# Reordering the filler projections of a hybrid RWKV-7 / neighbourhood-attention / MoE block on one Trainium2 core

## Chip, cores and metric

The kernel runs on one core of one Trainium2 chip. The metric is device time in microseconds of one execution; the median of three runs is compared. The engines are named as in the profile: PE (TensorE, matmul), PEld (its weight loads), DVE (VectorE), ACT (ScalarE), POOL (GpSimd), SP (SyncE, which here only issues DMAs).

## What is computed

One encoder layer on 512 tokens of width 1024, in float32:

```
h = rmsnorm(x)
p = h @ w_in                       # 1024 x 5504: r k v and low-rank columns of RWKV, q k v of attention, gate logits
y_a = rwkv7_bidirectional(...) @ w_o_rwkv      # 8 heads of 64, both directions
y_b = neighbourhood_attention_2d(q, k, v) @ w_o_na   # 8 heads of 64, grid 8 x 64, windows 8 x 16
x = x + (sig(g_a) * y_a + sig(g_b) * y_b) @ w_out
x = x + moe(rmsnorm(x))            # top group of 4, top 2 of its 8 experts, 32 experts
```

q and k of the attention are normalised per head (a root mean square over 64 columns, times a gain) before they are used. v and the gate logits are not.

## The kernel before, in words

**Stages.** Normalisation and the first projections; RWKV for head group 0 (`prep(0)`, which ends with the inversion of a 32x32 triangular system per chunk, `invert`), the chain of 16 chunk steps of group 0 (`chain(0)`); the same for group 1; neighbourhood attention in 8 blocks (two halves of the heads, 4 column blocks, each worked in two halves `hh`); the gated output projections (`out_gated`, `out_rows`); routing; 16 passes over pairs of experts. The experts' weights, 96 matrices of 1 MB, are loaded from the output projection on.

**The projections.** `w_in` is cut into 43 column tiles of 128. Fifteen are for RWKV. The other 28 are "others" (line 762), numbered m: 0 to 3 are q, 4 to 7 are k, 8 to 11 are v, 12 to 27 are gates. `proj` (line 304) makes one: a 512 KB weight load on SP, a split of the weights into a high and a low part (ACT writes w_hi, POOL or DVE writes w_lo; two buffers of each), and 24 matmuls of 128x512 (three for each of 8 slices) into one PSUM bank, called mm or x. Then comes what the kind of the tile asks for:

- q and k, `na_qk` (line 779): ACT squares the bank (osq) and copies it (oth), PE sums by heads into bank x, DVE takes a reciprocal square root in some twelve small operations (ngx, nrs_i, nst), spreads it (osq), PE transposes it into bank x, DVE multiplies, SP stores the tile to DRAM (d_q, d_k).
- v, `na_v` (line 800): ACT copies in three pieces, PE transposes into bank x, ACT copies, SP stores (d_v).
- gates: one ACT Tanh (oth<-mm,hb), SP stores (d_oth), line 559.

**What sets the order.** A tile framework schedules the program at compile time: each engine gets its instructions in one fixed order. The matmuls of these 28 tiles are given the lowest priority (`LOW`), what follows them the highest. Among themselves they come in the order of the program text, since weight buffers and banks are handed out in that order. `OTH` says how many are written where, `others(n)` (line 762) writes the next n: OTH[4] just ahead of the first inversion (line 745), OTH[0] after `prep(0)` (749), then the six inputs of RWKV group 1 (`GIN`, 751), OTH[1] ahead of the first chain (752), OTH[2] after the second inversion, alternating two banks (759), one after each of the first OTH[3] blocks of attention (835), and what is left after the attention, again in two banks (836).

**Who uses the results.** The attention fetches q, k and v of one half of the heads from DRAM (`na_inputs`, line 818), and its first products go into bank x (line 871), which is a single buffer. The output projection fetches the RWKV output ya, the attention output yb and the gates from DRAM; for its first 24 products (`add(m, c, range(2))`, line 961) it needs neither the second half of the heads nor the gates.

Of the kernel before, what the change touches and what calls it, by code (L numbers as in the profile page):

```python
# [23 lines left out]
HB = C // 2  # L24


OTH = (5, 8, 2, 10, 3)
GIN = [("k", 2), ("r", 2), ("v", 2), ("k", 3), ("r", 3), ("v", 3)]
WARM = 12
NX = 2  # L30
# [151 lines left out]
class K:  # L182
# [550 lines left out]
    def rwkv(self):  # L733
# [7 lines left out]
        def inputs(nm, q):  # L741
            self.rwkv_input(nm, q)
            if (nm, q) == ("v", 1):
                self.rwkv_lora(2, LOW)
                self.others(OTH[4])

        for _ in self.prep(0, inputs):
            pass
        self.others(OTH[0])
        for nm, q in GIN:  # L750
            self.rwkv_input(nm, q, LOW // 2)
        self.others(OTH[1])
        self.chain(0)
# [3 lines left out]
        for _ in p:  # L757
            pass
        self.others(OTH[2], ("mm", "x"))


    def others(self, n, banks=("mm",)):

        self.pbanks = banks
        for m in range(self.done, min(self.done + n, 28)):
            ps = self.proj(15 + m, LOW)
            t = self.rp.tile([P, T], F32, name="oth", tag="oth", bufs=2)
            with self.low(-LOW):
                if m < 8:
                    self.na_qk(m, ps, t)  # L770
                elif m < 12:
                    self.na_v(m, ps, t)
                else:
                    self.act(t, ps, AF.Tanh, scale=0.5, bias=self.hb[:, 4 + m:5 + m])
                    self.gate[m - 12] = self.spill(t, "oth%d" % m)
            self.done += 1
        self.pbanks = ("mm", "x")
# [50 lines left out]
    def na_attention(self):  # L828
        self.yb = [self.dram.tile([P, 2, 4, P], F32, name="d_yb%d" % i) for i in range(2)]
        for h4 in range(2):  # L830
            self.na_inputs(h4)
            for b in range(4):
                self.na_block(h4, b)
                if 4 * h4 + b < OTH[3]:
                    self.others(1)
# [616 lines left out]
```

## Time and profile before

| | |
|---|---|
| runs | 930.82, 932.72, 933.47 us; median 932.72 us |
| the profiled execution | 931.2 us |
| its span, first to last instruction | 929.4 us |
| mean granted clock of TensorE | 0.949 |
| busy: PE, DVE, ACT, POOL | 814.1, 433.4, 308.9, 181.5 us |

The times of stages in the trace: first inversion about 125 to 160 us, first chain 153 to 268 us, preparation of group 1 to 358 us, second inversion 358 to 390 us, second chain 383 to 490 us, attention 427 to 526 us, output projection from 562 us, experts from 685 us.

How to read the profile: "busy" is the time in which an engine has an instruction running; PE's durations are modelled, so a busy PE is not PE at its peak. A wait is idle time of an engine just before an instruction, with the instruction that ended it; "issue" is idle time for which the trace shows no releaser. The granted clock is a share of 2.4 GHz: 1.00 is that level and 0.50 the 1.2 GHz level, and a mean between is a mix in time of the two.

### The profile page before, as it was taken

The page shows a single profiled execution, that of the slowest core. Times are in us where ns is not written, and L with a number is a line of the kernel's source. Part 1 is how long each engine was busy: PE and PEld are TensorE (multiplying, and loading weights), DVE is VectorE, ACT ScalarE, POOL GpSimd, SP SyncE. Part 2 cuts the span into 40 slices and gives each one's busy share as a digit, 9 for nine tenths or more (in the row PEclk, how much of TensorE's full clock was granted, in tenths as well). Part 3 has the DMA queues.
Part 4 walks back from the last instruction along what each step waited for, and adds up shares of the span by engine and source line. Part 5 has one row for each costly group of instructions (what it writes and reads, how often), then busy time and mean ns, then how long its engine had stood idle before and what let it go on. Part 6 is the DMA issues. An engine that isn't in the chain of part 4 may idle for free. (4 is left out here: it accounts for less than half of the span.)

```text
span 929.4 us, 17293 instructions
## 1 busy us (share of the span) xinstructions
PE 814.1 (88%) x7192; PEld 529.8 (57%) x7192; DVE 433.4 (47%) x870; ACT 308.9 (33%) x667; POOL 181.5 (20%) x161
## 2 busy tenths in 40 slices
PE   8999887889987987799999999999669999888784
PEld 7676555556666765566666677878533333333331
DVE  5798984565689587224436505643612111111010
ACT  6454531123433553034756722223211111111110
POOL 2611121120003142123312230003321121211010
PEclk9999996899999999599999999999779999999998
DMA  6311130212112311422224548889989999999982
GB/s 216 110 59 47 35 102 26 68 58 69 36 59 81 125 53 62 140 72 67 81 68 137 182 135 287 300 326 380 353 330 410 394 345 395 395 393 400 398 341 44
DMA packets 49263, 176.18 MB, mean 190 GB/s; under 512 B 7584, under 2 KB 14368, under 8 KB 37152
## 3 DMA queue, kind: packets, MB, share of 16 engines
q1 hardware_dynamic: 43936, 164.56, 48.1%
q0 software_dynamic: 5248, 10.50, 4.2%
q8 instruction: 57, 0.93, 0.4%
q14 instruction: 22, 0.18, 0.1%
HBM read 159.30 MB, written 24.12 MB: 197 GB/s over the span
## 5 line engine op out<-in xcount | busy, mean ns | idle before, releaser
L203 PE MATMUL G<-ws,xT 128*64 128x512 f32 x512 | 128.9, 600 | 5.1 <-DMA ws<-in_wgu 3.8
L203 PE MATMUL mm<-hT_hi,w_lo 128*128 128x512 f32 x264 | 113.9, 432 | 7.9 <-ACT oth L188 6.8
L191 POOL TENSOR_TENSOR w_lo<-w_raw,w_hi 128x1024 fp32r<-128x1024 f32 x29 | 70.6, 2436 | 237.2 <-ACT w_hi L188 213.8
L203 PE MATMUL mm<-hT_hi,w_hi 128*128 128x512 f32 x264 | 112.0, 424 | 0.0
L203 PE MATMUL mm<-hT_lo,w_hi 128*128 128x512 f32 x264 | 111.2, 421 | 0.0
L203 PEld LDWEIGHTS G<-ws,xT 128*64 128x64 f32 x512 | 44.5, 138 | 77.7 <-issue 65.3
L203 PE MATMUL Yd<-ws,hT 128*64 128x512 f32 x256 | 65.7, 606 | 9.7 <-ACT y L188 8.7
L188 ACT ACTIVATE w_hi<-w_raw 128x1024 fp32r<-128x1024 f32 x59 | 62.2, 1055 | 30.5 <-PE mm L203 29.4
L203 PEld LDWEIGHTS mm<-hT_hi,w_lo 128*128 128x128 f32 x264 | 51.9, 197 | 26.2 <-issue 15.3
L191 DVE TENSOR_TENSOR w_lo<-w_raw,w_hi 128x1024 fp32r<-128x1024 f32 x30 | 37.7, 1257 | 50.1 <-ACT w_hi L188 50.1
L203 PEld LDWEIGHTS mm<-hT_lo,w_hi 128*128 128x128 f32 x264 | 51.8, 196 | 12.7 <-issue 2.0
L203 PEld LDWEIGHTS mm<-hT_hi,w_hi 128*128 128x128 f32 x264 | 52.0, 197 | 11.3 <-issue 1.5
L191 DVE TENSOR_TENSOR sg<-sg,G 128x256 f32<-128x256 f32 x16 | 6.7, 421 | 96.9 <-ACT sg L188 96.9
L1382 POOL DMA_INDIRECT out<-y,idx x16 | 25.2, 1577 | 117.3 <-DVE y L198 100.4
L198 DVE TENSOR_SCALAR y<-Yd,wts 128x512 f32<-128x512 f32 (+1 forms) x16 | 11.7, 734 | 77.1 <-PE Yd L203 62.6
L188 ACT ACTIVATE sg<-G,wts 128x256 f32<-128x256 f32 x16 | 7.6, 474 | 118.0 <-PE G L203 118.0
L651 DVE COPY R<-c 32x128 f32<-32x128 f32 x64 | 18.7, 293 | 52.6 <-ACT R L188 52.0
L203 PE MATMUL c<-R,T 128*32 128x64 f32 (+1 forms) x992 | 36.8, 233 | 7.2 <-DVE nrs_i L194 2.2
L203 PEld LDWEIGHTS c<-R,T 128*32 128x32 f32 (+1 forms) x992 | 26.6, 126 | 26.3 <-issue 14.0
L203 PE MATMUL tp<-T,KB 64*64 64x128 f32 x512 | 35.2, 281 | 7.3 <-ACT T L188 7.1
L203 PEld LDWEIGHTS Yd<-ws,hT 128*64 128x64 f32 x256 | 16.6, 136 | 43.5 <-ACT y L188 21.6
L188 ACT ACTIVATE T<-tp 64x256 f32<-64x256 f32 x64 | 23.9, 378 | 44.6 <-DVE T L191 43.6
(313 smaller groups left out, 1474.5 us busy)
## 6 DMA issues: line engine op xcount, KB each, us to landing
ws<-in_wgu SPq DMA_DIRECT2D x64, 1024.0 KB, 21.1
ws<-in_wd SPq DMA_DIRECT2D x30, 1024.0 KB, 21.2
w_raw<-in_w_in SPq DMA_DIRECT2D x43, 512.0 KB, 3.6
d_oth<-oth SPq DMA_DIRECT2D x16, 256.0 KB, 2.0
w_raw<-in_wo SPq DMA_DIRECT2D x8, 512.0 KB, 3.9
w_raw<-in_w_out SPq DMA_DIRECT2D x8, 512.0 KB, 5.9
x_in<-in_x SPq DMA_DIRECT2D x4, 512.0 KB, 5.4
ga<-d_oth SPq DMA_DIRECT2D x8, 256.0 KB, 4.0
```

Source lines behind the costliest of these rows:

```text
L188: self.nc.scalar.activation(out, in_, func, **kw)
L191: (eng or self.nc.vector).tensor_tensor(out, a, b, op=op)
L198: self.nc.vector.tensor_scalar(out, a, s1, None, op0=op0)
L203: return self.nc.tensor.matmul(out, l, r, start=start, stop=stop, **kw)
L651: self.nc.vector.tensor_copy(R[u, :, blk, p2], ps[u, 2:4])
L1382: self.nc.gpsimd.indirect_dma_start(out=self.A["out"], out_offset=bass.IndirectOffsetOnAxis(ap=idx, axis=0), in_=y, in_offset=None, bounds ...
```

## The change

The order of the 28 tiles is given by a list, and the five numbers differ: nine gates (12 to 20) first, then q, k and v (0 to 11), then the last seven gates. Written ahead of the first inversion: 3 as before; after `prep(0)`: 6 in place of 5; ahead of the first chain: 7 in place of 8; after the second inversion: 5 in place of 2; one after each of the first 7 blocks of attention in place of 8 blocks and 2 after it. So before, the places hold q0-q2; q3, k4-k7; v8-v11, g12-g15; g16, g17; g18-g25; g26, g27. After, they hold g12-g14; g15-g20; q0-q3, k4-k6; k7, v8-v11; g21-g27; none.

```diff
-OTH = (5, 8, 2, 10, 3)
+OTH = (6, 7, 5, 7, 3)
+
+TURN = list(range(12, 21)) + list(range(12)) + list(range(21, 28))
...
     def others(self, n, banks=("mm",)):
 
         self.pbanks = banks
-        for m in range(self.done, min(self.done + n, 28)):
+        for m in TURN[self.done:self.done + n]:
             ps = self.proj(15 + m, LOW)
```

## Rows read from the trace of the kernel before

**Rows 1.** The page, its second part: the granted clock of TensorE in 40 equal slices of the span, in tenths (9 is 90% or more).
```profile
PEclk9999996899999999599999999999779999999998
```

**Rows 2.** Busy time by stretch: the stretch and its length in us, then busy us and count of instructions of PE, PEld, DVE, ACT and POOL, the mean granted clock, the mean busy share of the DMA engines, GB/s.
```profile
125.00:160.00 35.00, 25.18 (x611) 18.65 (x609) 19.46 (x61) 7.88 (x14) 2.60 (x2) 0.78 0.20 70
145.00:165.00 20.00, 15.69 (x423) 11.98 (x425) 6.26 (x18) 3.44 (x7) 2.36 (x1) 0.50 0.13 42
165.00:227.00 62.00, 54.51 (x634) 37.51 (x634) 35.08 (x105) 17.47 (x42) 7.09 (x3) 0.97 0.18 57
290.00:358.00 68.00, 57.47 (x538) 42.35 (x537) 49.50 (x83) 33.61 (x82) 18.77 (x10) 0.95 0.25 79
358.00:397.00 39.00, 27.61 (x643) 20.14 (x646) 19.45 (x40) 6.31 (x12) 8.26 (x12) 0.69 0.34 111
370.00:390.00 20.00, 11.49 (x541) 9.71 (x542) 7.42 (x8) 1.47 (x3) 3.63 (x8) 0.50 0.50 162
397.00:427.00 30.00, 28.62 (x349) 19.12 (x342) 7.75 (x23) 10.37 (x25) 7.14 (x3) 1.00 0.25 80
526.00:562.00 36.00, 32.86 (x142) 25.95 (x140) 6.51 (x5) 10.58 (x16) 11.82 (x5) 1.00 0.50 163
```

**Rows 3.** Waits of PE from 125 to 160 us: who waited for whom, us in total, times, longest us.
```profile
PE c L203 <- issue: 5.4, 4, 2.3
PE x L206 <- DVE TI L191: 2.6, 1, 2.6
PE x L203 <- ACT osq L188: 1.1, 2, 0.7
```

**Rows 4.** The same from 160 to 227 us.
```profile
PE c L203 <- DVE nrs_i L194: 2.2, 1, 2.2
PE x L206 <- DVE osq L410: 2.1, 1, 2.1
PE c L203 <- DVE nrs_i L191: 1.5, 1, 1.5
...
PE x L203 <- ACT osq L188: 0.7, 1, 0.7
```

**Rows 5.** The same in four later stretches: the first row from 290 to 358 us, the next two from 358 to 397, the fourth from 397 to 427, the last from 526 to 562.
```profile
PE x L206 <- ACT oth L188: 2.6, 4, 0.8
...
PE c L203 <- DVE MT L605: 4.8, 1, 4.8
...
PE mm L203 <- ACT oth L188: 1.8, 2, 0.9
...
PE mm L203 <- ACT oth L188: 1.4, 2, 0.9
...
PE mm L203 <- ACT oth L188: 2.7, 3, 0.9
```

**Rows 6.** Busy time by stretch again, of the instructions alone that write or read the tile nrs_i: DVE, then granted clock, DMA share, GB/s.
```profile
160.00:227.00 67.00, 16.76 (x56) 0.93 0.19 60
```

**Rows 7.** ACT's copies of X, one in each step of a chain: first those from 160 to 227 us, then those from 397 to 427 us. Count, shortest/median/longest ns, first and last start, shape.
```profile
L188 ACT ACTIVATE X<-c x9: 277/277/278, 169.2 to 221.3; 128x128 f32<-128x128 f32 x9
...
L188 ACT ACTIVATE X<-c x5: 268/277/278, 403.1 to 423.9; 128x128 f32<-128x128 f32 x5
```

**Rows 8.** The tile oth: ACT's reads of q, k and v tiles, its reads of gates in bank mm, and SP's later fetches of the first eight gates. Columns as in rows 7.
```profile
L188 ACT ACTIVATE oth<-mm x20: 208/491/592, 116.0 to 342.3; 128x512 f32<-128x512 f32 x8, 128x64 f32<-128x64 f32 x8, 128x384 f32<-128x384 f32 x4
...
L188 ACT ACTIVATE oth<-mm,hb x14: 667/687/688, 360.6 to 561.6; 128x512 f32<-128x512 f32 x14
...
L563 SPq DMA_DIRECT2D ga<-d_oth x8: 319/327/549, 529.4 to 601.0; - x8
```

**Rows 9.** The attention's products of q and k. Columns as in rows 7.
```profile
L203 PE MATMUL x<-kT,qT x128: 218/272/373, 426.9 to 509.7; 64*128 64x128 f32 x96, 64*128 64x64 f32 x32
```

**Rows 10.** PE in order of time: the first matmul of two gate tiles beside the second chain, with one tile between them. Start us, us, engine, line, operation, out<-in, idle time before.
```profile
398.80 0.47 PE L203 MATMUL mm<-hT_hi,w_lo 128*128 128x512 f32 x1 [0.87 <-ACT oth L188]
...
417.01 0.50 PE L203 MATMUL x<-hT_hi,w_lo 128*128 128x512 f32 x1
```

**Rows 11.** In order of time, of several engines: the store of the last attention block, the end of its split on DVE, the first product of the output projection, the first two requests for expert weights. Columns as in rows 10.
```profile
526.27 0.56 SPq L907 DMA_DIRECT2D d_yb<-yb  x1
...
532.85 2.42 DVE L191 TENSOR_TENSOR yb_lo<-yb_f,yb_hi 128x256 fp32r<-128x256 f32 x1 [3.12 <-ACT yb_hi L188]
...
562.39 0.50 PE L203 MATMUL mm<-ya_lo,w_hi 128*128 128x512 f32 x1 [0.83 <-ACT oth L188]
...
564.94 0.91 SPq L1269 DMA_DIRECT2D ws<-in_wgu  x2
```

**Rows 12.** In order of time, of DVE and POOL: the start of the first inversion, a split of weights on POOL and the operation of the inversion that it met, and the like in the second inversion.
```profile
128.07 0.18 DVE L191 TENSOR_TENSOR pr<-NT,TI 128x30 f32<-128x30 f32 x1
...
133.43 2.40 POOL L191 TENSOR_TENSOR w_lo<-w_raw,w_hi 128x1024 fp32r<-128x1024 f32 x1 [9.73 <-ACT w_hi L188]
...
133.46 2.52 DVE L191 TENSOR_TENSOR pr<-NT,TI 128x126 f32<-128x126 f32 x1
...
362.59 2.37 DVE L191 TENSOR_TENSOR TI<-TI,pr 128x126 f32<-128x126 f32 x1
```

## The prediction, before the changed kernel was run

> **What bounds the kernel now.** I read the slices of the page first: TensorE (PE) is busy in nine tenths or more of almost every slice up to the expert part, and the granted clock of TensorE leaves full speed in three places, the two inversions and the routing [rows 1]. So in the part that the change touches, from about 93 us (the first projection of q) to 562 us (the first product of the output projection), PE is the bound, and what can be won there is idle time of PE and time at the lower clock. The table by stage [rows 2] shows where these are. Beside the second chain alone (397 to 427) PE is busy 28.62 of 30 us, and in the last 36 us before the output projection 32.86, with VectorE (DVE) busy only 6.51: there it works off the last gates and nothing else. The two inversions are the poor stages: 25.18 of 35 us and 27.61 of 39 us, at mean clocks of 0.78 and 0.69; from 145 to 165 and from 370 to 390 the granted clock was 0.50, which is the 1.2 GHz level.
>
> Then I read PE's waits stage by stage. From 125 to 227 us they are mostly ended by the small vector work of the q and k tiles: osq and nrs_i are the normalisation of a q or k tile [rows 3, 4]. With tiles that have no such work (v from 290 on, gates from 358 on), PE waits for ScalarE to read the one bank, oth, about 0.5 to 0.9 us a tile, and once 4.8 us in the second inversion for MT [rows 5]. DVE spends 16.76 us from 160 to 227 on the tile nrs_i alone, for some six q and k tiles [rows 6]: 2.8 us each, stretched by GpSimd. The chain shows the same: nine steps lie between 169.2 and 221.3 us, 6.5 us a step; five lie between 403.1 and 423.9, 5.2 us a step, with gates beside them [rows 7].
>
> **What the change moves.** All 28 projections stay, with all their matmuls, weight loads, splits and stores; only order and places in the program text change. The matmuls have the lowest priority, so the split into places decides little by itself: the tiles flow in their written order into whatever PE has free, through one queue of weight buffers. Before, q and k are read out from 116 us, the v tiles up to 342.3, and gates from 360.6 to 561.6 [rows 8]. After, nine gates come first, then the six inputs of the second group, then q, k, v, and the last seven gates beside the attention.
>
> Term 1, q and k leave the first inversion and chain: the waits on osq and nrs_i go, 1.1 and 2.2 + 2.1 + 1.5 + 0.7, so **-7.6 us** [rows 3, 4]. The 2.6 us on TI I don't count: PE would then stand at MT, as in the second inversion [rows 5]. What is late next there is the inversion itself on DVE. It starts at 128.07 [rows 12], and before it DVE worked on a q tile; an earlier start helps only if PE has nothing else, so zero, hidden by the projections beside it; if these ran out it would be worth up to the 2.8 us of a tile.
>
> Term 2, gates in their place: ScalarE's read ends 1.4 us of waits in 397 to 427, over three tiles, 0.47 each; eight tiles give **+3.7 us** [rows 5].
>
> Term 3, clock: from 165 to 227 it was 0.97 on the mean, so 3.7 us at the lower level, which cost about half their work, **-1.7 us**; bounds 0 and -1.7 [rows 2].
>
> Term 4, seven q and k tiles into 290 to 397, where v and gates stand now. The trace has no such tile there. The nearest rows give 0.55 us a tile (1.1 us for two tiles in the first inversion) and 1.27 (7.6 for six) [rows 3, 4]; I take 0.9, since DVE has 18.5 of 68 us idle from 290 to 358 [rows 2] and takes the 2.8 us a tile only with delay. That is 6.3 us, less the 2.6 and 1.8 us that PE waits there for oth now [rows 5]: **+1.9 us**, bounds -0.6 and +4.5.
>
> Term 5, one k and four v tiles beside the second chain in place of gates: v waits 2.6 us over four tiles against 1.4 for the gates [rows 5], **+1.2 us**. Two banks in turn instead of one save such a wait for every other tile and cost it for the next, since v itself uses bank x for its transposes: zero.
>
> Term 6, no gates after the attention: of the three waits of 0.9 us in 526 to 562 I drop two [rows 5], **-1.8 us**. The six tiles worked off there don't become free, they cost PE the same 5.7 us each earlier.
>
> The queues: 28 weight loads and stores on SP keep their spacing; the gates' stores come early and are read only from 529.4 on [rows 8], at no cost, with all of the chain between. The stores of the last q, k and v tiles now come just before SP's fetches of qT, kT and vtok; before, v's last tile was read out at 342.3 and the attention began at 426.9 [rows 8, 9]. Each fetch waits for its store, and behind it on SP stand the weight loads of the gates. Bounds 0 and 8 us; I take 0, because the projections of the chain and the chain itself cover it. The splits on GpSimd number the same.
>
> The start of the attention moves: it needs bank x, which the last tile written ahead of it holds. That was the 18th of the 28 and is now the 21st. Two tiles beside the chain started at 398.80 and 417.01 with one between, 9.1 us a tile [rows 10]; three more are 27 us, so about 454, less what is won before, 450. PE does the same work in another order, so I count nothing, with the chain's later steps as the cover; if the attention itself should end last, this is the price (second rival).
>
> Sum: -7.6 + 3.7 - 1.7 + 1.9 + 1.2 - 1.8 = **-4.3 us**. What follows 562 shifts with it: the first expert weights are requested at 564.94, just after the last gate [rows 11]. The profiled execution took 931.2 us (span 929.4 and 1.8 around it), the median of the runs shown is 932.72, 1.5 more; 931.2 - 4.3 + 1.5 = **928.4 us**. Its own range, by the bounds, is 924 to 933.
>
> **A rule that speaks against it.** Beside the first inversion an operation of 128x126 took 2.52 us while a split of weights ran on GpSimd from 133.43 for 2.40 us; in the second the same happened at 362.59 (2.37) [rows 12]. The page "SBUF — State Buffer" of the Trainium skill, section "SBUF: two separate sides", says that a DVE operation with two SBUF inputs and a GpSimd one that reads SBUF exclude each other, the later one blocking until the other ends; the trace agrees. By that rule one more split beside each inversion would add two such blocks, some 2.1 us each, and the sum would be about 0. I count none, since the number of splits that fall into an inversion follows from how fast PE works off tiles, not from the text.
>
> **Rivals.** (a) No change: the waits move with the tiles. Term 4 at its upper bound and term 3 at zero: -7.6 + 3.7 + 4.5 + 1.2 - 1.8 = 0, 932.7 us. For it: DVE is busier from 290 to 358 (0.73) than from 165 to 227 (0.57) [rows 2]. Against: the second part of the chain there has its own slack.
>
> (b) Slower: the attention ends last. It took from 426.9 to the last store at 526.27, 99 us [rows 9, 11]. From 454 it ends at 553; with a fetch of 8 us and the three further gates taking 3 us of it, 564. The last block must then go through DRAM and be split, which took from 526.27 to 535.27, 9 us [rows 11]; the output projection has 24 products that don't need it, about 6 us at 36 us for 142 matmuls [rows 2, 11]. So it decides from where the last store comes after 559 (562.39 + 6 - 9): at 564 it costs 5 to 6 us, 938.5 us. For it: 142 matmuls, six gates of 24, cover this tail now [rows 2], few or none after. Against: PE would have finished the gates by then, so the attention would have PE to itself.
>
> (c) Faster by far: the inversions fill. If gates keep PE busy where it stood at MT (4.8 us) and at TI (2.6) [rows 3, 5] and the clock stays up in both stretches of 20 us (busy 15.69 and 11.49 us at half speed, so up to 13 us; I take half, since small matmuls remain) [rows 2], this gives a further 14 us, 914.5 us. Against: in the second inversion gates were already there, and PE stood all the same, its queue being in order; 5.4 us of the first are ended by issue, not by missing work. The page "TensorE: Matmul & The Clock Gate", section "What's actually happening", of the Trainium skill says that the clock follows how busy PE has been; the trace agrees, with 0.50 granted right after these idle stretches.
>
> That the change does not do what it says is part of (a): the low priority can let the tiles run at nearly the old times.
>
> **How the numbers follow.** Forecast 0.42, (a) 0.24, (b) 0.20, (c) 0.14. About 0.3% (2.8 us) is what a measurement of this kernel can tell from no change. Faster: three quarters of the forecast, all of (c), a tenth of (a), 0.48. Same: the rest of the forecast, most of (a), a tenth of (b), 0.30. Slower 0.22. The range reaches half into (c) and past (b): 916 to 940.
>
> **What the profile of after should show.** No wait of PE ended by nrs_i or osq before 227 us; first-chain steps near 5.2 us; the q and k work of DVE between 270 and 400; in the second inversion still a wait on MT; the attention's first product at 440 to 455; its last store before 559; and the output projection's first product at about 558. A first chain that stays at 6.5 us a step, or a last store after 559, would prove me wrong.

## The result, and the profile after

The changed kernel took 941.83 us, the median of four runs (940.18 to 947.41), beside 933.1, the median of four, for the kernel before: a ratio of 1.0116, 95% interval 1.0074 to 1.0158. So it is slower by 1.2%; 928.4 had been predicted, in 916 to 940. Its profiled run is its slowest: 947.41 us, 5.6 over its median, so what the two traces differ by (16.2 us) is about twice what the medians do (8.7). Runs over 1.5% above the fastest of their kernel (two of "six gates 18, DVE splits", one of "before, low q/k") count in the medians below, but not in the ratios. In the changed kernel lines up to 27 keep their numbers, those behind stand two further down (L203 is L205).

First the granted clock, to be laid beside [rows 1]: the low slice of the first inversion (6 in the seventh place, at 139 us) is now an 8; the one slice of 5 in the second inversion (372 to 395 us) has become a trough: of the six slices from 284 to 426 us one shows 8 and four show 7.

```profile
PEclk9999898999998797779999999999969999999999
```

Busy time by stretch in the changed kernel, columns as in [rows 2].

```profile
125.00:160.00 35.00, 26.42 (x655) 19.34 (x653) 17.48 (x41) 6.90 (x14) 4.78 (x2) 0.85 0.23 78
145.00:165.00 20.00, 17.46 (x380) 12.03 (x380) 5.32 (x13) 6.19 (x14) 4.35 (x2) 0.89 0.21 69
165.00:227.00 62.00, 59.52 (x702) 38.80 (x702) 25.14 (x58) 22.49 (x52) 7.59 (x4) 1.00 0.25 82
290.00:358.00 68.00, 59.39 (x505) 43.03 (x504) 50.07 (x129) 27.60 (x55) 13.23 (x9) 0.90 0.12 40
358.00:397.00 39.00, 26.94 (x641) 19.79 (x640) 17.70 (x45) 4.46 (x11) 6.21 (x10) 0.65 0.26 84
...
397.00:427.00 30.00, 23.07 (x227) 16.57 (x226) 15.57 (x43) 6.76 (x16) 4.73 (x2) 0.83 0.18 62
526.00:562.00 36.00, 36.00 (x204) 25.87 (x202) 14.35 (x29) 26.19 (x73) 10.65 (x18) 1.00 0.37 117
```

The first chain gained what it should: PE is busy 59.52 of 62 us at full clock (54.51 at 0.97 before). The loss stands in the second inversion and above all in the second chain: 23.07 of 30 us at 0.83, where PE had 28.62 at 1.00.

Three long stretches sum this up. The same view, first of the kernel before, then of the changed one:

```profile
93.00:270.00 177.00, 154.24 (x2057) 107.89 (x2059) 119.27 (x293) 60.19 (x130) 21.22 (x14) 0.90 0.18 58
270.00:430.00 160.00, 135.24 (x1896) 98.69 (x1884) 96.14 (x179) 58.37 (x134) 39.23 (x26) 0.90 0.27 86
430.00:526.00 96.00, 90.59 (x1069) 63.98 (x1058) 47.95 (x110) 64.64 (x191) 23.30 (x45) 1.00 0.33 99
```

```profile
93.00:270.00 177.00, 156.75 (x2299) 110.01 (x2299) 107.82 (x211) 66.20 (x136) 28.51 (x18) 0.95 0.22 71
270.00:430.00 160.00, 130.57 (x1503) 95.58 (x1504) 99.53 (x251) 47.68 (x107) 28.84 (x22) 0.81 0.20 66
430.00:526.00 96.00, 89.15 (x1063) 62.19 (x1061) 37.77 (x92) 48.18 (x142) 24.68 (x31) 0.95 0.32 96
```

How to read them: idle time of PE is the length less its busy time; time at the 1.2 GHz level is twice the length times what the clock lacks to 1 (at a mean of 0.81, 2 x 160 x 0.19 = 61 us). Up to 270 us the change wins 2.5 us of idle time and 18 us of low clock; from 270 to 430 it loses 4.7 and 29, from 430 to 526 it loses 1.4 and 10. The price of a microsecond at low clock can be had from two kernels of one order: the fastest version found below starts the output projection at 534.07 us, the kernel before at 562.39 [rows 11]. In these stretches it has 13.6 us less idle time and 37 us less low clock (its rows are below); (28.3 - 13.6) / 37 = 0.4, an estimate. With it the change gains 10 us up to 270 us, loses 16 in the next stretch and 5 in the third: 12 us. From 526 to 562 us it wins 3 back (PE busy 36.00 us against 32.86), so the estimate accounts for some 9 of the 15.9 us by which its output projection starts later; the rest is open.

PE's waits in the changed kernel: from 125 to 160 us, from 160 to 227, from 358 to 397 and from 397 to 430.

```profile
PE c L205 <- issue: 3.7, 3, 1.8
PE c L205 <- DVE MT L607: 3.4, 1, 3.4
PE mm L205 <- ACT oth L190: 1.2, 2, 0.9
...
PE c L205 <- DVE R L193: 3.1, 5, 0.6
...
PE c L205 <- issue: 5.2, 3, 2.4
PE c L205 <- DVE nst L196: 3.3, 1, 3.3
...
PE c L205 <- DVE nst L202: 3.1, 1, 3.1
PE c L205 <- DVE R L653: 2.9, 1, 2.9
```

Beside [rows 3, 4]: before 227 us no wait on osq or nrs_i is left. The waits on nst, the same normalisation, now stop the products of the second inversion and chain (bank c).

The copies of X, one a step, in the same two stretches as [rows 7]:

```profile
L190 ACT ACTIVATE X<-c x12: 267/272/278, 162.9 to 222.2; 128x128 f32<-128x128 f32 x12
...
L190 ACT ACTIVATE X<-c x3: 278/278/278, 400.3 to 421.2; 128x128 f32<-128x128 f32 x3
```

The first chain's steps: 59.3 us for eleven, 5.4 each (6.5 before). The second's: 20.9 us for two, 10.4 each (5.2 before). All 16 copies of the second chain, before and after:

```profile
L188 ACT ACTIVATE X<-c x16: 256/277/278, 383.3 to 484.7; 128x128 f32<-128x128 f32 x16
...
L190 ACT ACTIVATE X<-c x16: 277/278/302, 375.1 to 488.2; 128x128 f32<-128x128 f32 x16
```

So the second chain starts 8.2 us earlier than before, takes 113.1 us instead of 101.4, and ends 3.5 us later. Beside it stand the last three of the four k tiles, as their stores show, and all four v tiles:

```profile
394.72 0.33 SPq L800 DMA_DIRECT2D d_k<-oth  x1
...
409.72 0.32 SPq L800 DMA_DIRECT2D d_k<-oth  x1
...
426.32 0.32 SPq L800 DMA_DIRECT2D d_k<-oth  x1
```

The attention's products of q and k, as in [rows 9]:

```profile
L205 PE MATMUL x<-kT,qT x128: 218/272/576, 467.4 to 556.3; 64*128 64x128 f32 x96, 64*128 64x64 f32 x32
```

And in order of time, as in [rows 11], the store of its last block, the first product of the last gate tile, and the first of the output projection:

```profile
566.11 0.51 SPq L909 DMA_DIRECT2D d_yb<-yb  x1
...
571.79 0.47 PE L205 MATMUL mm<-hT_hi,w_lo 128*128 128x512 f32 x1 [0.87 <-ACT oth L190]
...
578.30 0.50 PE L205 MATMUL mm<-ya_lo,w_hi 128*128 128x512 f32 x1 [0.83 <-ACT oth L190]
```

The attention starts 40.5 us later than before, the output projection 15.9. One of the long steps of the second chain, from 400.34 to 407.70, in order of time over the engines:

```profile
400.34 0.28 ACT L190 ACTIVATE X<-c 128x128 f32<-128x128 f32 x1 [3.08 <-PE c L205]
...
400.67 0.60 ACT L190 ACTIVATE osq<-mm 128x512 f32<-128x512 f32 x1
401.16 0.59 ACT L190 ACTIVATE oth<-mm 128x512 f32<-128x512 f32 x1
...
401.64 1.06 ACT L190 ACTIVATE w_hi<-w_raw 128x1024 fp32r<-128x1024 f32 x1
...
402.73 0.27 ACT L190 ACTIVATE R<-c 32x128 f32<-32x128 f32 x1
402.78 2.39 POOL L193 TENSOR_TENSOR w_lo<-w_raw,w_hi 128x1024 fp32r<-128x1024 f32 x1 [11.70 <-ACT w_hi L190]
...
402.82 2.37 DVE L202 TENSOR_SCALAR nst<-nrs_i 128x8 int32<-128x8 int32 x1
...
406.43 0.30 DVE L653 COPY R<-c 32x128 f32<-32x128 f32 x1
...
407.36 0.29 DVE L653 COPY R<-c 32x128 f32<-32x128 f32 x1
...
407.70 0.45 PE L205 MATMUL c<-R,T 128*64 128x64 f32 x8 [2.93 <-DVE R L653]
```

Three things stand between the chain's X and its R: on ACT the k tile's two reads and the next tile's w_hi; on DVE an operation of eight columns that began 0.04 us after GpSimd's split and ended with it; behind it the tile's remaining small operations. PE worked on a tile meanwhile, ran out at 404.8, and stood 2.93 us.

### The profile page after: what moved, and what is told of

Same layout as the page of the kernel before. It is cut to its first block, busy times and chain, and to the rows that moved or that the text cites. A ratio compares the mean times of both kernels' runs of the same rounds, so it can differ in the third digit from the quotient of the medians.

```text
span 945.6 us, 17302 instructions
## 1 busy us (share of the span) xinstructions
PE 828.3 (88%) x7192; PEld 536.3 (57%) x7192; DVE 426.6 (45%) x870; ACT 310.2 (33%) x667; POOL 181.1 (19%) x161
## 5 line engine op out<-in xcount | busy, mean ns | idle before, releaser
L205 PE MATMUL G<-ws,xT 128*64 128x512 f32 x512 | 129.9, 601 | 5.8 <-DMA ws<-in_wgu 4.4
L205 PE MATMUL mm<-hT_hi,w_lo 128*128 128x512 f32 x264 | 113.3, 429 | 4.0 <-ACT oth L190 3.7
L205 PE MATMUL mm<-hT_hi,w_hi 128*128 128x512 f32 x264 | 112.8, 427 | 0.0
L205 PE MATMUL mm<-hT_lo,w_hi 128*128 128x512 f32 x264 | 111.7, 423 | 0.0
L205 PEld LDWEIGHTS G<-ws,xT 128*64 128x64 f32 x512 | 44.6, 138 | 79.3 <-issue 65.0
L205 PE MATMUL Yd<-ws,hT 128*64 128x512 f32 x256 | 65.7, 606 | 9.7 <-ACT y L190 8.6
L205 PEld LDWEIGHTS mm<-hT_hi,w_lo 128*128 128x128 f32 x264 | 51.9, 196 | 18.2 <-issue 5.2
L205 PEld LDWEIGHTS mm<-hT_hi,w_hi 128*128 128x128 f32 x264 | 51.9, 196 | 13.2 <-issue 3.2
L205 PEld LDWEIGHTS mm<-hT_lo,w_hi 128*128 128x128 f32 x264 | 51.6, 195 | 12.0 <-issue 2.0
L205 PE MATMUL c<-R,T 128*32 128x64 f32 (+1 forms) x992 | 37.7, 236 | 13.5 <-DVE R L653 4.9
L205 PE MATMUL tp<-T,KB 64*64 64x128 f32 x512 | 41.6, 310 | 7.2 <-ACT T L190 7.2
L205 PEld LDWEIGHTS c<-R,T 128*32 128x32 f32 (+1 forms) x992 | 27.5, 129 | 35.7 <-DVE R L653 14.1
L205 PEld LDWEIGHTS tp<-T,KB 64*64 64x64 f32 x512 | 33.6, 153 | 18.3 <-ACT T L190 11.7
```

Of the source, the lines that this page charges most:

```text
L205: return self.nc.tensor.matmul(out, l, r, start=start, stop=stop, **kw)
```

## The experiments

All 18 further kernels, of 5 to 12 runs each, beside the two. The ratio is to the kernel before on the same chip, with its interval. PE's busy time and the clock are read from the profiled run, in stretches as above; the last column is the attention's first product.

| kernel | median us | ratio | PE busy, clock 93-270 | 270-430 | attention |
|---|---|---|---|---|---|
| before | | 1 | 154.2, 0.90 | 135.2, 0.90 | 426.9 |
| after | 941.8 | 1.0116 (1.0074-1.0158) | 156.8, 0.95 | 130.6, 0.81 | 467.4 |
| six gates, 18 ahead | 922.0 | 0.9912 (0.9888-0.9936) | 158.6, 0.95 | 135.6, 0.89 | 419.3 |
| three gates, 18 ahead | 926.2 | 0.9972 (0.9944-1.0001) | 157.1, 0.94 | 141.5, 0.90 | 416.1 |
| six gates, 21 ahead | 933.0 | 1.0043 (1.0015-1.0071) | 156.5, 0.94 | 137.0, 0.90 | 439.9 |
| old order, 21 ahead | 933.2 | 1.0027 (1.0005-1.0049) | 149.0, 0.91 | 137.5, 0.90 | 444.2 |
| gates, v first, 21 ahead | 932.8 | 1.0045 (1.0016-1.0075) | 157.0, 0.95 | 138.9, 0.86 | 471.2 |
| after, no rsqrt | 929.5 | 0.9986 (0.9965-1.0006) | 157.8, 0.95 | 139.7, 0.85 | 453.5 |
| before, no rsqrt | 926.3 | 0.9965 (0.9939-0.9991) | 157.2, 0.91 | 136.8, 0.91 | 421.4 |
| after, low q/k | 927.7 | 0.9993 (0.9970-1.0016) | 157.1, 0.95 | 140.9, 0.85 | 461.5 |
| before, low q/k | 929.2 | 0.9962 (0.9930-0.9995) | 153.0, 0.87 | 135.9, 0.93 | 429.3 |
| six gates 18, low q/k | 928.2 | 0.9977 (0.9957-0.9996) | 157.8, 0.93 | 134.0, 0.84 | 439.5 |
| six gates 21, low q/k | 943.7 | 1.0157 (1.0127-1.0187) | 155.6, 0.89 | 134.5, 0.85 | 455.9 |
| after, DVE splits | 913.2 | 0.9818 (0.9787-0.9849) | 159.2, 0.93 | 139.6, 0.93 | 440.9 |
| before, DVE splits | 911.8 | 0.9782 (0.9755-0.9808) | 159.4, 0.96 | 139.4, 0.90 | 408.2 |
| six gates 18, DVE splits | 913.7 | 0.9775 (0.9728-0.9821) | 160.1, 0.95 | 144.3, 0.95 | 406.3 |
| six gates 21, DVE splits | 930.6 | 1.0005 (0.9987-1.0022) | 157.8, 0.93 | 133.8, 0.87 | 443.9 |
| after, pieces | 923.8 | 0.9927 (0.9904-0.9951) | 156.7, 0.95 | 135.8, 0.88 | 449.9 |
| before, pieces | 912.7 | 0.9803 (0.9773-0.9833) | 155.5, 0.91 | 144.4, 0.96 | 408.9 |
| before, DVE splits and pieces | 902.8 | 0.9695 (0.9674-0.9717) | 161.4, 0.95 | 143.0, 0.96 | 399.2 |

**Order and places.** The theories that the expectations name: L, the attention starts late, behind 21 tiles instead of 18; Q, the q and k work now lies beside the second inversion and chain. The edits, on the kernel after, in short:

```diff
+TURN = [12..17] + [0..11] + [18..27]   # six gates first; three gates: [12..14] + [0..11] + [15..27]
 OTH = (5, 8, 2, 10, 3)                 # 18 ahead, as before
-OTH = (5, 8, 2, 10, 3)
+OTH = (6, 7, 5, 7, 3)                  # 21 ahead, as after: with six gates, or with the old order
+TURN = [12..20] + [8..11] + [0..7] + [21..27]   # gates, v first: then q, k
```

Six gates, 18 ahead: 

> Six gates first, then q, k, v, then ten gates, with the five numbers of the kernel before: 18 tiles stand ahead of the attention, the same 18 as before, only their order differs. Theory L (late attention: what costs is that 21 tiles instead of 18 stand ahead of the attention, whose first product slid from 427 to 467 us): the attention begins at 420 to 430 us again and the time is that of before, 933 us, or a little under, since the first chain keeps its 5.1 us a step. Theory Q (what costs is where the q and k work falls: beside the preparation of group 1, the second inversion and the second chain): as slow as the changed kernel, 938 to 943 us, and second-chain steps next to a k tile of 8 to 13 us.

Old order, 21 ahead: 

> The five numbers of the changed kernel with the natural order of the tiles (q, k, v, gates): 21 tiles ahead of the attention, q and k beside the first chain as before. Theory L: 940 to 943 us, the attention's first product some 25 to 40 us later than 427. Theory Q: 931 to 935 us, as before, although the attention begins later; second-chain steps near 5.2 us.

Six gates, 21 ahead: 

> Six gates first, then q, k, v, then ten gates, with the five numbers of the changed kernel: 21 tiles ahead of the attention, but q and k come three tiles earlier than in the changed kernel. Theory Q (what costs is q and k work that reaches the second inversion and the second chain): no q or k tile lies there, so the time stays near that of the same order with 18 ahead, 922 to 926 us, with second-chain steps near 5.2 us until the attention joins. Theory L (the late attention costs, and costs more with gates first): 932 us or more.

Gates, v first, 21 ahead: 

> The changed kernel with the four v tiles ahead of q and k: nine gates, v, q, k, seven gates. So four more q and k tiles reach the second inversion and chain, none fewer stand ahead of the attention. Theory Q: slower than the changed kernel, by 2 to 4 us for each of these four tiles as far as it shows, 945 to 957 us; more second-chain steps of 8 to 13 us. Theory L: as the changed kernel, 938 to 943 us, since the attention waits for the same 21 tiles.

Three gates, 18 ahead: 

> Three gates first, then q, k, v, then thirteen gates, with the five numbers of the kernel before: q and k leave the first inversion but stay beside the first chain. Theory Q and the prediction's first term (the first chain gains by having no q and k beside it): between before and six gates first, 924 to 930 us; first-chain steps 6 to 7 us once q begins, as before. If only the first inversion counts: as six gates first, 921 to 923 us.

The old order with 21 ahead came out as Q expected, six gates with 21 ahead as L did, three gates within 924 to 930; six gates with 18 ahead (922.0) and v first (932.8) are faster than either theory had it. Gates ahead of q and k are good by themselves: 0.9912 with six of them, a third of that with three. 21 tiles ahead cost 0.3% in the old order and 1.3% with six gates. Against Q: with v ahead of q, more q and k tiles lie beside the second chain than after the change, and this kernel is the faster of the two (1.0045), although its attention starts at 471.2. Its second chain takes as long (355.7 to 466.9 us), but starts 19 us earlier. So neither the count of q and k tiles there nor the late attention alone gives 1.2%.

**The q and k work itself.** In two kernels the eleven small operations of the reciprocal square root are left out, so q and k are scaled by something else; in four others the work behind a q or k tile is no longer scheduled ahead of everything.

```diff
-        self.rsqrt_bits(st, x, shape, "nrs_i")
+        st = x                                   # no rsqrt
...
-            with self.low(-LOW):
+            with self.low(LOW // 4 if m < 8 else -LOW):   # low q/k
```

After, no rsqrt: 

> The changed kernel without the eleven small vector operations of the reciprocal square root of each q and k tile (q and k are scaled by the mean square itself). To be compared with the kernel before with the same left out. Theory Q: most of the loss of 9 us is gone, so 929 to 934 us, and within 3 us of its counterpart; no step of the second chain over 8 us. Theory L: still some 8 us slower than its counterpart, attention still from 450 us or later.

Before, no rsqrt: 

> The kernel before without the same eleven small vector operations of each q and k tile. Both theories: a little faster than before, 926 to 931 us, by the waits of TensorE on nrs_i and osq beside the first chain (some 7 us by the trace of before) as far as they lie on the path. It is the counterpart from which the other kernel without them is measured.

After, low q/k: 

> The changed kernel with the epilogues of q and k tiles (copies, sums, reciprocal root, scaling, store) at a low instead of the highest priority, so that the chain's own copies are placed ahead of them. Theory Q in its sharper form (a k tile costs because its work stands in the engines' queues ahead of the chain's step): second-chain steps beside k tiles fall from 8 to 13 us to 6 to 8, time 930 to 936 us. If the cost is the work itself, or the blocking of VectorE by GpSimd, the time stays at 938 to 943 us. Theory L: no change or slower, as q and k are finished later and the attention with them.

Before, low q/k: 

> The kernel before, order and places untouched, with the same lower priority of the q and k tiles' vector work alone. Theory Q: the first chain's steps fall from 6.5 to about 5.2 us and its end comes 10 to 20 us earlier; time 924 to 930. Theory L: the attention's first product stays within 10 us of 427, so the time stays within 2 us of 933. If q and k come so late that the tiles behind them wait, 933 to 938.

Six gates, 18 ahead, low q/k: 

> Six gates first, the attention behind 18 tiles (922.0 us, ratio 0.991 to before), and now the vector work of the q and k tiles no longer has the highest priority but stands behind that of the chains and of the preparation. Theory Q (the loss comes where this work stands ahead of a step of the chain or of the preparation): its steps of 8 to 12 us between 190 and 250 fall to about 5 to 6, and the kernel gains a further 2 to 7 us, 915 to 920. Theory L (the late start of the attention alone decides): the attention starts as in the kernel with six gates, at 415 to 425, and the time stays within 2 us of 922.

Six gates, 21 ahead, low q/k: 

> Six gates first but the attention behind 21 tiles (933.0 us, ratio 1.004), with the lower priority of the q and k work. No q or k tile stands beside its second chain. Theory L: the attention still starts behind 21 tiles, at 435 to 445, PE again has thin stretches in 470 to 526, and it stays 6 us or more behind the same edit at 18 tiles: 925 to 932. Theory Q alone: the two come out within 3 us of each other, 915 to 922.

Without the eleven operations the change costs 0.2% (0.9986 against 0.9965) instead of 1.2%: nearly all of the loss goes with this work. The edit isn't clean, though: without these operations, others of DVE and PE's products also come in another order. The lower priority took 14 us off the kernel after and 0.4% off the kernel before, which leaves 0.3% between them, and added 6 and 11 us to the two with six gates. Neither of these two came out within an expectation, nor did the 927.7 (930 to 936). It is a reshuffle whose sign changes with the order; that the priority is the cause is not shown.

**Who writes w_lo, and in what pieces.** The step shown above has a DVE operation shut out by a split on GpSimd. One edit gives the splits of the eight q and k tiles to DVE, the other cuts GpSimd's splits into eight pieces.

```diff
-        ... self.wload(m, eng=self.nc.gpsimd if m >= 15 else None)
+        ... self.wload(m, eng=self.nc.gpsimd if m >= 23 else None)   # DVE splits
...
-        self.tt(lo, raw, hi, OP.subtract, eng=eng)
+        for w in 8 column slices (one if eng is None):                # pieces
+            self.tt(lo[:, w], raw[:, w], hi[:, w], OP.subtract, eng=eng)
```

After, DVE splits: 

> The kernel after with one change: the low part of the weights of the 8 q and k tiles is written by DVE instead of GpSimd, so that no operation of DVE can be shut out by these eight splits. If the shutting out (2.4 us each beside the chain's step at 402.8) makes the long steps of the second chain: steps beside k tiles fall from 8 to 13 us to 6 or 7, and the time falls by 3 to 8 us, to 934 to 939. If the order on DVE and ACT does it (the tiles' work ahead of the chain's copies), whoever writes the low part: the eight splits of about 1.1 us now stand on DVE itself, steps stay at 7 us or more, and the time stays between 940 and 945.

After, pieces: 

> The kernel after; every split that GpSimd writes (w_lo) is written in eight pieces of 128 columns instead of one of 1024, on the same engine and at the same place in the text. Theory P (a whole split shuts out a small DVE operation for 2.2 us and more; this costs the time): what an operation can lose falls to a piece, about 0.3 us, although GpSimd is busy no shorter; most of what the splits on DVE gave comes here too, 914 to 930. Theory O (the gain with the splits on DVE came from another order of the instructions on DVE and GpSimd, or from less work on GpSimd): 938 to 950, since GpSimd has the same or more work.

Before, DVE splits: 

> The kernel before with the low parts of the 8 q and k tiles written by DVE. In its trace the operations of DVE that ran beside GpSimd lost 9.8 us against their own shortest from 125 to 230 us and 12.7 from 230 to 430 (kernel after: 2.2 and 25.9; with the splits on DVE 2.3 and 5.9). Theory P: the loss of the first stretch goes, the later one stays with the v and gate tiles, for which GpSimd still splits; 8 splits of 1.1 us come onto DVE: 4 to 10 us faster, 920 to 926. Theory O: within 3 us of 930.

Six gates, 18 ahead, DVE splits: 

> Six gates first, the attention behind 18 tiles (922.0, ratio 0.991), with the q and k tiles' low parts on DVE. Its DVE operations lost 13.4 us beside GpSimd from 230 to 350. Theory P: 6 to 12 us faster, 909 to 916, ratio 0.977 to 0.987. If the early start of the attention adds to that (theory L), it is faster than the kernel after with the same edit (913.2, 0.982); if it does not, the two are within 3 us.

Six gates, 21 ahead, DVE splits: 

> Six gates first, the attention behind 21 tiles (933.0, ratio 1.004), with the q and k tiles' low parts on DVE; lost beside GpSimd: 9.4 us from 230 to 350, 5.4 after. Theory P: 5 to 8 us faster, 921 to 926. Theory L, on top: 6 us or more behind the same edit with the attention behind 18 tiles.

Before, pieces: 

> The kernel before with every split on GpSimd written in eight pieces. The same edit took the kernel after from 941.8 to 923.8 (0.9927 of before). If the loss of the change is that more of these lockouts fall where they end TensorE's waits (25.9 us of lost DVE time from 230 to 430 us after the change, 12.7 before), the same edit gives the kernel before less, 5 to 10 us, and the two come out within 4 us of each other, 920 to 926. If the change loses by something else as well (the late attention), the kernel before gains as much as the kernel after did, 12 to 20 us: 911 to 919.

Before, DVE splits and pieces: 

> The kernel before with the low parts of the q and k tiles on DVE and the other splits on GpSimd in eight pieces, so that neither kind of tile can shut out an operation for long. With the first alone 911.8 (0.978); its trace still shows 10.0 us of DVE time lost beside GpSimd from 230 to 430. If that still ends waits of TensorE: 904 to 909. If what remains is hidden: within 2 us of 912. If the eight pieces, which keep GpSimd and the shared port busy half as long again, disturb more than the whole split did: 914 to 919.

No expectation held the first of these, 913.2, nor the 911.8 of the old order, which gains more than was expected (920 to 926); with six gates and 18 ahead the same edit came out as expected (0.9775, its runs scattered from 903.6 to 921.1), with 21 ahead it gave only 2 us (5 to 8 had been expected) and left this kernel 2.3% behind the one with 18 ahead, as theory L expected. Whether the early start of the attention adds to the edit, as L has it, stays unclear: by the medians six gates with 18 ahead and the kernel after are level (913.7 and 913.2), by the ratios 0.4% apart, with intervals that overlap. What the splits did to a small operation is seen in one row for each of three kernels (after; pieces; DVE splits), from 270 to 430 us: the first bit operation of the reciprocal square root, once a tile, with its shortest, median and longest time in ns.

```profile
L687 DVE TENSOR_SCALAR nrs_i<-ngx x8: 158/960/2372, 283.0 to 417.9; 128x8 int32<-128x8 int32 x8
```

```profile
L690 DVE TENSOR_SCALAR nrs_i<-ngx x8: 166/212/433, 279.6 to 403.2; 128x8 int32<-128x8 int32 x8
```

```profile
L687 DVE TENSOR_SCALAR nrs_i<-ngx x8: 157/171/179, 286.6 to 392.3; 128x8 int32<-128x8 int32 x8
```

The longest of eight falls from 2.37 us to 0.43 and 0.18. The stores of the four q tiles show what it does to a tile's turn; the same three kernels:

```profile
L800 SPq DMA_DIRECT2D d_q<-oth x4: 319/320/320, 292.5 to 354.0; - x4
```

```profile
L803 SPq DMA_DIRECT2D d_q<-oth x4: 319/320/320, 287.8 to 341.5; - x4
```

```profile
L800 SPq DMA_DIRECT2D d_q<-oth x4: 319/319/320, 295.6 to 340.8; - x4
```

Three tiles take 61.5 us, 53.7 and 45.2. The pieces decide between the rivals of that run. GpSimd is busier (45.48 us against 28.84 from 270 to 430), and the order is the old one: without the splits, DVE's 841 operations and GpSimd's 133 come in the same order in both traces, with pieces and without; so do ACT's 663 and PE's 7192 matmuls in the kernel before (in the kernel after some 2 and 220 of them moved). Nor do PE's products start sooner: from 93 to 600 us PE waits for no w_lo in the two kernels with whole splits. Yet the pieces made the kernels 18 and 17 us faster: being shut out for the length of a split is a cost, and a large one, about 2%. The splits on DVE are less clean, since they move 221 of DVE's operations in the kernel after and 341 in the one before.

But it is not what the change lost. The pieces took 2.0% off the kernel before as well (0.9803, the second value of its expectation), so after is still 1.3% behind (0.9927). The traces show why: from 93 to 530 us, 16 operations of DVE took over 1 us more beside GpSimd than the shortest of their line, tiles and shape in the kernel before, 12 after the change, and one in each with the pieces. The change moved the lockouts and did not add any. The DVE splits took off 3.0% and 2.2%; the gap shrinks to 0.4%. With them the attention starts 33 us later after the change than before it (440.9 and 408.2), for that 0.4%; but with six gates and the same edit, 38 us (443.9 and 406.3) go with 2.3%, so this doesn't bound theory L.

Both edits together give the fastest version, a little below its first expectation: the lockouts that remained with the first edit still cost something. Its busy time from 93 to 270 us, from 270 to 430 and from 430 to 526, and then, in order of time, its output projection's first product:

```profile
93.00:270.00 177.00, 161.43 (x2229) 113.09 (x2227) 120.67 (x309) 64.45 (x138) 12.72 (x23) 0.95 0.21 66
270.00:430.00 160.00, 142.97 (x1961) 103.34 (x1952) 93.91 (x199) 71.29 (x184) 54.97 (x111) 0.96 0.28 86
430.00:526.00 96.00, 89.28 (x923) 65.49 (x919) 35.13 (x85) 55.61 (x145) 36.71 (x86) 1.00 0.42 133
```

```profile
534.07 0.50 PE L203 MATMUL mm<-ya_lo,w_hi 128*128 128x512 f32 x1 [0.83 <-ACT oth L188]
```

902.84 us, 3.1% under the kernel before, with the old order and places: up to 430 us PE stands idle 15 us less than in the kernel before (7.2 and 7.7 in the two stretches), and its clock from 270 on is 0.96.

## Why the prediction was wrong

Right: PE was the bound, with idle time and low clock as the things to win, and terms 1 to 3 came and more: in 125 to 160 and 165 to 227 us PE's idle time fell by 6.3 us, where terms 1 and 2 had 3.9. PE stood at MT in the first inversion (3.4 us), as term 1 said. Waits on osq and nrs_i left the first chain; its steps fell to 5.4 us; the gates waited less than the 3.7 us forecast (1.2 from 125 to 227 us); and the first inversion gained clock that I had not counted in the forecast (145 to 165 us: 0.50 to 0.89). Term 6 came by its number and not by its reason: PE was busy all 36 us from 526 to 562, but the attention was still running there, and behind it stood gates all the same, with the two waits on oth that I had dropped (0.87 and 0.83 us).

**The step that failed is the price of the q and k tiles at their new place, terms 4 and 5**, forecast at +1.9 and +1.2 us. From 270 to 430 us the changed kernel lost 4.7 us of PE's time and 29 us to the low clock, 16 us in all by the estimate above. By stretch, with the same estimate: 290 to 397, the place of term 4, cost 2.7 us, inside its bounds, and all of it by the clock; 397 to 427, the place of term 5, cost 9.6 (5.6 us of idle time and 10 of low clock); about 4 fall between 270 and 290, at a clock of 0.74 (1.00 before), where the forecast had no term. (The upper bound of term 4 was a little high: the 7.6 us for six tiles hold the 1.1 of the first inversion; 6.5 give 1.08 a tile and +3.2.)

Three things were wrong. I had one k tile beside the second chain; there were three. I had taken 0.9 us a tile from PE's waits beside the first chain; but beside the second a step took 10.4 us instead of 5.2, where the first chain's had cost 6.5 instead of 5.4, and the second inversion's products waited 3.3 us on nst, where I expected a wait on MT. And I gave PE's thin stretches no price in clock outside the inversions: term 3 counted what leaves, nothing counted what comes.

The length of the second chain (its 16 copies of X) goes with the gap between the two orders in each of five pairs: 113.1 us after and 101.4 before without an edit (1.2%), 108.5 and 98.7 with the pieces (1.3%); 102.1 and 101.7 with the splits on DVE (0.4%), 99.1 and 101.0 with the low priority (0.3%), 103.2 and 101.3 without the reciprocal square root (0.2%). That is a match, not a proof: the three edits that close the gap also reorder the engines' work, so which property of the q and k work makes the steps long stays open.

**The rule that I weighed was right, and I applied it to too few operations.** I asked whether a further split would fall into an inversion, and counted none. In [rows 6] I had the 2.8 us a tile "stretched by GpSimd" and moved it as if only PE's turn at the end of a tile could feel it. The experiments showed that these lockouts cost about 2%, but the kernel before as much as the kernel after; they are not what the forecast missed. The Trainium skill, page "SBUF — State Buffer", section "SBUF: two separate sides", counts operations of DVE in a 2-port mode among those that can be shut out, beside those with two SBUF inputs. The trace agrees so far that an operation with one input of eight columns took 2.37 us beside a split; no run here shows its mode.

**The start of the attention**, counted as nothing, came at 467.4 instead of 440 to 455. The zero is not borne out: three more tiles ahead of the attention cost 0.3% in the old order, and 1.3 to 2.3% with six gates first. How much of the change's 1.2% is of this kind is not shown, since no run has nine gates first and fewer than 21 tiles ahead. The rival built on it (the attention ends last) had the right sign and nearly the time, 938.5 us, but not the mechanism: the last store came at 566.11, past its 559, and yet the output projection waited for the last gate (578.30, 0.83 us on oth), with PE working off gates up to there. Of rival (c) a part came: the first inversion's clock rose (125 to 160: 0.78 to 0.85), though PE still stood 8.6 of 35 us; the second did not fill (358 to 397: 0.65, 0.69 before).

**Open.** It is not settled why the splits on DVE close most of the gap between the two orders, where the pieces leave it as it was, though both take lockouts away (nine are left before and six after with the splits on DVE). The DVE time lost beside GpSimd is no measure of the gap: the expectations had 25.9 us against 12.7 from 230 to 430 us; counted again from the traces (each operation beside one of GpSimd, its time less the shortest of its line, tiles and shape) it is 20.2 against 12.4, and from 125 to 230 us 2.2 against 9.8, so that the sums are equal. Nor is it settled why six gates with 21 ahead stay 1.3 to 2.3% behind six gates with 18 under every edit; the second chain starts later there (384.0 and 377.9 us), and the clock from 270 to 430 is 0.87 against 0.95 with the splits on DVE.

## What to carry to other kernels

A filler tile is not only its matmuls: before it is moved, ask which engine's small operations come with it, and whose steps stand behind them at the new place. Price a stretch in which PE gets thin by the clock as well as by the waits, from rows of the same kernel at either level. And where GpSimd and DVE both work on SBUF, cut GpSimd's long operations into pieces or give them to DVE before tuning the order: here that was worth 3%, the order 1%, and with the splits on DVE six gates first added nothing to the old order (0.9775 and 0.9782).

## What was not expected of the hardware

A DVE operation of 128x8 elements that takes 0.16 us took up to 2.37 us beside a GpSimd split of 2.39 us. Eight pieces make such a split longer (3.87 us for the eight at one place, 2.39 in one), and the kernels got 17 to 18 us faster. The same split on DVE takes 1.22 us. And a microsecond at the 1.2 GHz level cost about 0.4 us of the end, over stretches in which PE was busy 0.85 to 0.94 of the time.
